# A hybrid decoder trunk on one core: the S5 stage's step list rewritten, with the gates and the first output products taken into it

## The chip, the cores and the metric

The kernel runs on one NeuronCore of a Trainium2 chip. The metric is device time in microseconds (us) of one execution; smaller is better. A core has five engines that run their own instruction queues in order: PE (TensorE, matrix products), ACT (ScalarE), DVE (VectorE), POOL (GpSimd) and SP (SyncE, which here only issues DMAs). They wait for one another through semaphores.

## What is computed

Two layers on a sequence of 256 tokens with 1024 channels, float32 throughout. Each layer is half a SwiGLU feed-forward, a mixer, and another half feed-forward. The mixer of layer 0 is an S5 state-space layer, that of layer 1 a block-sparse attention. The change is in the S5 mixer, cut here to what matters:

```python
u = h @ w_in                                   # 256 x 1024
# per group of 16 channels: 64 complex states, a diagonal recurrence over the 256 tokens
st = scan(lam, bb * u)                         # st[t] = lam * st[t-1] + bb u[t]
y = Re(c * st) + d_skip * u
g = gelu(y)
g = g * sigmoid(g @ w_glu)
return g @ w_out
```

The kernel computes the recurrence on every fourth token only (the tokens in between are folded into small tables), as a rotation, a real scan and a rotation back.

## The kernel before

The program runs six phases one after the other: `f00`, `s5`, `f01` (layer 0), `f10`, `moba`, `f11` (layer 1). Large products keep their precision by a split: every operand is written as a high part in the fast format fp32r plus a low part (the remainder), and a product is three matmuls: high by high, high by low, low by high (`mm3`, L398 to 401).

**Weights** come through the class `Stream`. A unit is 128x2048 floats in one of three raw buffers (L176, L182, L188 issue the loads on SP). `split` (L74 to 97) turns a half unit of 128x1024 into `whi` on ACT (L86) and `wlo` on DVE (L87), for units with gains in two pieces (L92, L93). There are 9 slots of `whi` and `wlo`. A call of `pump` splits the next half if its raw unit has been asked for and a slot is free; else it does nothing. `release` gives a slot back. When both halves of a unit are split, its raw buffer is free and SP issues the next load. Which pump splits what is thus fixed when the program is written out; at run time ACT and DVE take the splits in their queues' order.

**The S5 phase** works on eight blocks b of 128 channels. Its steps, with their names in the step list:

- `w<c0>.<t>:<k>` is `w_in`: one of 8 contraction steps of a product u = h @ w_in for column group c0 (256 columns for c0 = 0 and 256, 512 for c0 = 512) and token half t. With k = 7, ACT copies the sum from PSUM to `us` (L999) and DVE transposes it into `U` (L1000).
- `t<b>` is `t1`: 32 matmuls of 63 columns (L1009) that make block b's inputs of the scan in PSUM: in bank A0 to A3 for b < 4, in one of the two M buffers for b of 4 and above.
- `r<b>` is `rot`: two small ACT instructions (L1020, L1021), then on DVE four rotation products in place in PSUM (L1028 to 1031) and two scans (L1033), then on POOL four instructions (L1035 to 1038) that rotate back into `hr`.
- `y<b>` is `y_out`: 48 matmuls (L1052) from `U` and `hr`, then the gelu on ACT (L1056) and a transpose on DVE (L1058).
- `g<b>` is `g_tr`: two PE transposes (L1067). For b of 2 and above ACT writes the high part (L1070), DVE the low part (L1071), and ACT then a plain copy `gf` (L1072).
- `u<b>:<o>` is `glu`: block b's part of g @ w_glu for eight column blocks o (L1090 in plain float32 for b < 2, three fp32r matmuls L1092 to 1094 for the others). The sums are in the banks A0 to A3, two column blocks in each.
- `P` is one pump; `gelu` and `sigmoid` load the ACT table of that function (L234); `x` is a part of the phase's entry.

The list itself is `plan` (L1139 to 1146), written out by hand or by a planner; `step` (L1117 to 1135) runs a word of it. The order of the words is the order in every engine's queue.

**After the list** comes fixed code: for i = 0 to 3, `glu(6)` and `glu(7)` for the column blocks 2i and 2i+1 and then `gate(i)`. A gate reads the sum in bank Ai with a sigmoid (ACT, L1103), multiplies (DVE, L1105), writes the high part (ACT, L1107) and the low part (DVE, L1108). Then come the output products `so(b, t, n)` (L1110 to 1115, by `bank_mm` and `mm3`) for b = 0 and 1, with one or two pumps after each pair. `so(0, t, n)` begins a new sum in bank A(2t+n), the bank that gate 2t+n reads; `so(b)` takes the gated blocks 2b and 2b+1 that gate b writes. The products with b = 2 and 3, the residual sum (L371) and the transposes for the next phase are in `boundary` (L373 to 397).

Of the kernel before, what the change touches and what calls it, by code (L numbers as in the profile page):

```python
# [120 lines left out]
def trunk_kernel(ctx: ExitStack, tc, x, ffn_norm, ffn_w_gate, ffn_w_up, ffn_w_down, mix_norm,  # L121
# [20 lines left out]
    def psA(i):  # L142
        return pp.tile([128, 512], F32, name=f"pA{i}", tag=f"A{i}", bufs=1)
# [12 lines left out]
    where = {}  # L156
# [74 lines left out]
    def warm(func):  # L231

        w = sp.tile([128, 1], F32, name="warm", tag="warm", bufs=1)
        nc.scalar.activation(w, ones[:, 0:1], func)  # L234
# [33 lines left out]
    if "s5" in phases:  # L268
        rho = cp.tile([128, 32], F32, name="rho")
        tstack, lstack, xstack = ExitStack(), ExitStack(), ExitStack()  # L270
# [8 lines left out]
    st = Stream(nc, units, rp, hp)  # L279
# [20 lines left out]
    XP = [xp]  # L300
# [22 lines left out]
    def prep(t, n, ph, sq=True):  # L323

        if (ph, "x") not in X:
            X.clear()
            X[ph, "x"] = True
            X["h"], X["l"] = home(XP[0], ph)
        hh = h[t][:, n * 512:(n + 1) * 512]
        ps = psR()  # L330
        pv = ps.rearrange("p (k c) -> p k c", c=128)
        for k in range(4):
            nc.tensor.transpose(pv[:, k, :], hh[:, k * 128:(k + 1) * 128], ident)  # L333
        xh, xl = (X[p][:, n * 4:n * 4 + 4, t * 128:t * 128 + 128] for p in "hl")
        nc.scalar.activation(xh, pv, AF.Copy)
        nc.vector.tensor_tensor(xl, pv, xh.bitcast(F32), op=OP.subtract)
        if sq:
            squares(t, n)
# [80 lines left out]
    def bank_mm(acc, t, n, lh, ll, u, kks, first, last):  # L419

        for kk in kks:
            wh, wl = st.get(u, kk)
            c = slice(n * 512, n * 512 + 512)
            mm3(acc[2 * t + n], lh[:, kk, t * 128:t * 128 + 128], ll[:, kk, t * 128:t * 128 + 128],
                wh[:, c], wl[:, c], first and kk == kks[0], last and kk == kks[-1])
# [536 lines left out]
    def s5(nxt, entry):  # L962
        V, P = nc.vector, nc.gpsimd
        HALVES = (slice(0, 64), slice(64, 128))
        wstack = ExitStack()
# [16 lines left out]
        def w_in(c0, t, k):  # L982

            n = 512 if c0 >= 512 else 256
            if k == 0:
                W[c0, t] = psM()
            ps = W[c0, t]
            ts = slice(t * 128, t * 128 + 128)
            u = where["win", c0 // 512, k // 4]
            i = (k % 4) // 2  # L990
            wh, wl = st.get(u, i)
            c = (k % 2) * 512 + c0 % 512
            mm3(ps[:, 0:n], X["h"][:, k, ts], X["l"][:, k, ts], wh[:, c:c + n], wl[:, c:c + n], k == 0, k == 7)
            left[u, i] = left.get((u, i), 4 * (512 // n)) - 1
            if not left[u, i]:
                st.release(u, i)
            if k == 7:
                us = wp.tile([128, 512], F32, name="us", bufs=1)
                nc.scalar.activation(us[:, 0:n], ps[:, 0:n], AF.Identity, scale=Rr[t])  # L999
                V.transpose(U[:, c0 // 32:(c0 + n) // 32, t, :], us[:, 0:n].rearrange("p (q c) -> p q c", c=32))  # L1000
# [73 lines left out]
        def glu(b, os):  # L1074

            u = where["glu", b // 2]
            g = gf[b // 2][:, b % 2, :]
            if b < WHOLE:
                w = st.raw[u][:, b % 2 * 1024:b % 2 * 1024 + 1024]
            else:  # L1080
                gh, gl = GT["h"][:, b, :], GT["l"][:, b, :]
                wh, wl = st.get(u, b % 2)
            for o in os:
                first, last = b == 0 and o % 2 == 0, b == NB - 1
                if first:
                    acc[o // 2] = psA(o // 2)
                d = acc[o // 2][:, (o % 2) * 256:(o % 2) * 256 + 256]
                c = slice(o * 128, o * 128 + 128)
                if b < WHOLE:
                    mm(d, w[:, c], g, start=first, stop=last, skip_group_check=True)  # L1090
                else:
                    mm(d, wh[:, c], gh, start=first, stop=False, skip_group_check=True)  # L1092
                    mm(d, wh[:, c], gl, start=False, stop=False, skip_group_check=True)
                    mm(d, wl[:, c], gh, start=False, stop=last, skip_group_check=True)
                if o == 7 and b >= WHOLE:
                    st.release(u, b % 2)
                elif o == 7 and b % 2:
                    st.free_raw(u)

        def gate(i):  # L1100

            sg = fp.tile([128, 2, 256], F32, name="sg", tag="gr", bufs=2)
            nc.scalar.activation(sg, acc[i].rearrange("p (a c) -> p a c", a=2), AF.Sigmoid)  # L1103
            g = gf[i]
            V.tensor_tensor(g, g, sg, op=OP.mult)  # L1105
            gh, gl = (GT[p][:, 2 * i:2 * i + 2, :] for p in "hl")
            nc.scalar.activation(gh, g, AF.Copy)  # L1107
            V.tensor_tensor(gl, g, gh.bitcast(F32), op=OP.subtract)  # L1108

        def so(b, t, n, last=False):  # L1110
            u = where["so", b]
            if b == 0:
                acc[2 * t + n] = psA(2 * t + n)
            gh, gl = (GT[p][:, 2 * b:2 * b + 2, :] for p in "hl")
            bank_mm(acc, t, n, gh, gl, u, [0, 1], b == 0, last)

        def step(word):  # L1117
            name, _, ks = word.partition(":")
            ks = [int(k) for k in ks.split("-")] if ks else []
            ks = range(ks[0], ks[-1] + 1) if ks else ()  # L1120
            if name[0] == "w":
                c0, t = name[1:].split(".")
                for k in ks:
                    w_in(int(c0), int(t), k)
            elif name[0] == "u":
                glu(int(name[1]), ks)
            elif name == "x":
                if entry:
                    prep(1, 1, "s5")
            elif name == "P":  # L1130
                st.pump()
            elif name in ("gelu", "sigmoid"):
                warm(AF.Gelu_apprx_tanh if name == "gelu" else AF.Sigmoid)
            else:
                {"t": t1, "r": rot, "y": y_out, "g": g_tr}[name[0]](int(name[1]))

        plan = """  # L1139
            w0.0:0-1 P x w0.0:2-5 P w0.0:6 w0.1:0 w0.0:7 w0.1:1-4 P w0.1:5-7 w256.0:0-4 w256.1:0-1 t0 w256.0:5  # L1140
            w256.1:2 P w256.0:6 r0 w256.1:3 w256.0:7 P t1 w512.0:0 w256.1:4-7 w512.0:1 r1 w512.0:2-3 t2 gelu
            r2 t3 y0 w512.0:4-5 w512.1:0-1 w512.0:6 w512.1:2 r3 w512.1:3-4 w512.0:7 w512.1:5 y1 w512.1:6-7 g0
            y2 P P u0:0-1 g1 t4 u0:2-3 r4 g2 u0:4 t5 u0:5-7 r5 u1:0 t6 y3 u1:1-2 r6 u1:3-7 u2:0-2 t7 y4 g3
            u2:3-5 r7 y5 u2:6-7 u3:0-2 y6 g4 u3:3-4 g5 u3:5-7 P u4:0 P u4:1 P u4:2 g6 y7 u4:3-4 P P u4:5-7
            u5:0-1 sigmoid g7 u5:2-5 P u5:6-7 P
        """
        for word in plan.split():
            step(word)
        wstack.close()
        lstack.close()  # L1150
        XP[0] = xstack.enter_context(tc.tile_pool(name="xt2", bufs=1))
        for i in range(4):
            glu(6, (2 * i, 2 * i + 1))
            glu(7, (2 * i, 2 * i + 1))
            gate(i)
        for b in range(2):
            for t in range(2):
                for n in range(2):
                    so(b, t, n)
                if t == 1:  # L1160
                    for i in range(2):
                        st.release(where["so", b], i)
                st.pump(2 - b * t)

        boundary(nxt, [lambda t, n: so(2, t, n), lambda t, n: so(3, t, n, True)], acc, 1.0, pumps=(1, 2))
        for b in (2, 3):
            for i in range(2):
# [204 lines left out]
    v2, rn, r2 = (sp.tile([128, 2], F32, name=n, tag=n, bufs=1) for n in ("ms2", "rn2", "rr2"))  # L1372
# [41 lines left out]
    for i, ph in enumerate(phases):  # L1414
        nxt = phases[i + 1] if i + 1 < len(phases) else None
        if ph[0] == "f":
            if i:
                with tc.tile_pool(name="rows", bufs=1) as RP[0]:
                    ffn_w(ph, nxt, entry_hooks(ph))
            else:  # L1420
                ffn(ph, nxt, first, fill, to_rows, to_columns)
            if i and phases[i - 1] == "s5":
                xstack.close()
        else:
            if ph == "s5":
                st.aged = False
                for _ in tab:
                    slot[0] += 2.0
                s5(nxt, i > 0)
            else:  # L1430
                moba(nxt)
# [43 lines left out]
```

## Time and profile before

| What | Value |
|---|---|
| Median of three runs | 982.28 us (981.8 to 982.3) |
| The profiled execution: its own time | 982.36 us |
| Its span, first to last instruction | 980.4 us, so 1.96 us lie around it |
| DVE busy in the span | 688.8 us (70%) |
| ACT busy in the span | 560.4 us (57%) |
| POOL busy in the span | 186.5 us (19%) |
| First w_in matmul of the S5 phase, by the timeline | 213.48 us |
| First matmul of so(0) | 287.14 us |

Times in the views are counted from the span's start. A row of the timeline reads: start, duration, engine, source line, operation, tile written and tiles read, how many instructions were merged; a bracket gives the idle time of the engine just ahead and what ended it. Matmuls overlap, so what one costs PE is the distance from its start to the next start, not its duration.

### The profile page before, as it was taken

The numbers are of one execution on the slowest core, as the hardware profiler recorded it, in microseconds if no ns is written. First come the engines' busy times: TensorE is split into PE (matmuls) and PEld (weight loads), VectorE is DVE, ScalarE is ACT, GpSimd is POOL, SyncE is SP. The second block draws the span as 40 slices with busy tenths as digits, with TensorE's granted clock in tenths as the row PEclk, the third lists the DMA queues.
The fourth block names the chain that finished last, engine by engine and source line by source line (L and its number), as shares of the span: only waits on it lengthen the run. The fifth ranks groups of instructions, "written<-read, shape, count | busy, mean of one in ns | idle before, by whom it ended". The sixth has DMA issues, their size and how long they took to land.

```text
span 980.4 us, 17231 instructions
## 1 busy us (share of the span) xinstructions
PE 972.2 (99%) x6727; PEld 867.5 (88%) x6727; DVE 688.8 (70%) x1118; ACT 560.4 (57%) x1008; POOL 186.5 (19%) x364
## 2 busy tenths in 40 slices
PE   9999999999999999999999999999999999999998
PEld 7878888788888999999999999998788899999997
DVE  5799767768768676666667766665789667766662
ACT  7565766553267555555456655544897556655540
POOL 6963544416511000000010000000441010000000
PEclk9999999999999999999999999999999999999999
DMA  8988877887645666565536656562544546656531
GB/s 284 249 269 279 275 261 242 298 324 245 252 173 182 213 208 215 172 212 175 172 125 214 221 173 214 173 215 92 172 145 157 186 143 214 231 174 213 172 130 44
DMA packets 140002, 198.74 MB, mean 203 GB/s; under 512 B 18232, under 2 KB 111504, under 8 KB 139664
## 3 DMA queue, kind: packets, MB, share of 16 engines
q1 hardware_dynamic: 133808, 184.32, 57.5%
q0 software_dynamic: 5536, 12.71, 3.6%
q8 instruction: 53, 0.87, 0.4%
q10 hardware_dynamic: 576, 0.61, 0.3%
q14 instruction: 29, 0.24, 0.1%
HBM read 183.89 MB, written 13.66 MB: 202 GB/s over the span
## 4 chain that ended last, share of the span: by engine, by line
PE 94%; DVE 2%; ACT 2%; issue 1%; POOL 1%; DMA 1%; SPq 0%; POOLq 0%; DVEq 0%; ACTq 0%
PE pM L554 13%; PE pM L553 13%; PE pM L555 13%; PE pA L399 9%; PE pA L401 9%; PE pA L400 9%; PE pM L399 6%; PE pM L400 6%; PE pM L401 6%; PE pA L473 1%; PE pR L1052 1%; PE pR L333 1%; DVE wlo L87 1%; PE pA L1090 1%; PE pR L866 1%
## 5 line engine op out<-in xcount | busy, mean ns | idle before, releaser
L553 PE MATMUL pM<-xa,whi 128*128 128x256 f32 x1056 | 295.7, 280 | 0.0
L554 PE MATMUL pM<-xa,whi 128*128 128x256 f32 x1056 | 294.9, 279 | 0.0
L555 PE MATMUL pM<-xa,wlo 128*128 128x256 f32 x1056 | 294.7, 279 | 0.0
L93 DVE SCALAR_TENSOR_TENSOR wlo<-raw,gT,whi 128x512 fp32r<-128x512 f32 x328 | 228.1, 748 | 71.2 <-ACT whi L92 71.0
L87 DVE TENSOR_TENSOR wlo<-raw,whi 128x1024 fp32r<-128x1024 f32 (+1 forms) x155 | 187.5, 1225 | 56.0 <-ACT whi L86 54.8
L92 ACT ACTIVATE whi<-raw,gT 128x512 fp32r<-128x512 f32 x328 | 213.7, 711 | 16.4 <-PE pA L401 14.6
L554 PEld LDWEIGHTS pM<-xa,whi 128*128 128x128 f32 x1056 | 198.5, 188 | 2.6
L553 PEld LDWEIGHTS pM<-xa,whi 128*128 128x128 f32 x1056 | 198.5, 188 | 2.3
L555 PEld LDWEIGHTS pM<-xa,wlo 128*128 128x128 f32 x1056 | 198.5, 188 | 0.0
L86 ACT ACTIVATE whi<-raw 128x1024 fp32r<-128x1024 f32 (+1 forms) x155 | 158.7, 1049 | 26.1 <-DMA raw<-in_ffn_w_up_dram 9.8
L399 PE MATMUL pA<-whi,ah 128*128 128x512 f32 x352 | 138.8, 394 | 0.0
L400 PE MATMUL pA<-wlo,ah 128*128 128x512 f32 x352 | 137.6, 391 | 0.0
L401 PE MATMUL pA<-whi,al 128*128 128x512 f32 x352 | 137.6, 391 | 0.0
L568 ACT ACTIVATE sg<-gr 128x256 f32<-128x256 f32 x66 | 27.6, 418 | 165.7 <-DVE gr L565 165.7
L399 PE MATMUL pM<-whi,xa 128*128 128x512 f32 (+1 forms) x304 | 122.2, 402 | 0.0
L400 PE MATMUL pM<-wlo,xa 128*128 128x512 f32 (+1 forms) x304 | 115.8, 381 | 0.1
L401 PE MATMUL pM<-whi,xa 128*128 128x512 f32 (+1 forms) x304 | 115.5, 380 | 0.0
L348 POOL TENSOR_TENSOR ms<-ss 128x1 f32<-128x1 f32 x10 | 1.9, 193 | 470.3 <-ACT sq L345 470.3
L401 PEld LDWEIGHTS pA<-whi,al 128*128 128x128 f32 x352 | 66.1, 188 | 14.3
L399 PEld LDWEIGHTS pA<-whi,ah 128*128 128x128 f32 x352 | 66.1, 188 | 11.6
L400 PEld LDWEIGHTS pA<-wlo,ah 128*128 128x128 f32 x352 | 66.2, 188 | 11.3
L565 DVE TENSOR_TENSOR gr<-pM,rrow 128x512 f32<-128x512 f32 x66 | 45.5, 689 | 40.9 <-PE pM L555 40.8
(269 smaller groups left out, 1214.5 us busy)
## 6 DMA issues: line engine op xcount, KB each, us to landing
raw<-in_ffn_w_down_dram SPq DMA_DIRECT2D x44, 1024.0 KB, 5.4
raw<-in_ffn_w_gate_dram SPq DMA_DIRECT2D x80, 512.0 KB, 4.0
raw<-in_ffn_w_up_dram SPq DMA_DIRECT2D x80, 512.0 KB, 5.1
raw<-in_moba_w_qkv_dram SPq DMA_DIRECT2D x12, 1024.0 KB, 5.1
TB<-dB SPq DMA_DIRECT2D x8, 768.0 KB, 6.6
raw<-in_ffn_w_gate_dram SPq DMA_DIRECT2D x16, 256.0 KB, 4.4
raw<-in_ffn_w_up_dram SPq DMA_DIRECT2D x16, 256.0 KB, 4.7
dB<-tt POOLq DMA_DIRECT2D x16, 256.0 KB, 5.1
```

Of the source, the lines that this page charges most:

```text
L86: nc.scalar.activation(hi[:, c], r[:, c], AF.Copy)
L87: nc.vector.tensor_tensor(lo[:, c], r[:, c], hi[:, c].bitcast(F32), op=OP.subtract)
L92: nc.scalar.activation(hi[:, c], r[:, c], AF.Identity, scale=g)
L93: nc.vector.scalar_tensor_tensor(lo[:, c], r[:, c], g, hi[:, c].bitcast(F32), op0=OP.mult, op1=OP.subtract)
L399: mm(o, xh, wh, start=start, stop=False)
L400: mm(o, xh, wl, start=False, stop=False)
L401: mm(o, xl, wh, start=False, stop=stop)
L553: mm(o, a, xh, start=k == 0 and i == 0, stop=False, skip_group_check=True)
L554: mm(o, a, xl, start=False, stop=False, skip_group_check=True)
L555: mm(o, b, xh, start=False, stop=k == 7, skip_group_check=True)
L565: V.tensor_tensor(gr, ps.rearrange("p (i c) -> p i c", i=2), Rr["row"][:, None, :].to_broadcast([128, 2, 256]), op=OP.mult)
L568: nc.scalar.activation(sg, gr[:, 0, :], AF.Silu)
```

## The change

The step list is rewritten, and two new words join it: `a<i>` runs `gate(i)` (before the first, two memory pools are closed and one is opened, as the fixed code did), and `o<b>:<k>` runs `so(b, k // 2, k % 2)`, with the release of its slots after k = 3. The fixed code for `glu(6)`, `glu(7)`, the gates and `so(0)`, `so(1)` goes, since these are words now. The code of every step is as it was, and each step runs as often as before. The whole of the diff:

```diff
             elif name == "P":
                 st.pump()
+            elif name[0] == "a":
+                if name == "a0":
+                    wstack.close()
+                    lstack.close()
+                    XP[0] = xstack.enter_context(tc.tile_pool(name="xt2", bufs=1))
+                gate(int(name[1]))
+            elif name[0] == "o":
+                b = int(name[1])
+                for k in ks:
+                    so(b, k // 2, k % 2)
+                    if k == 3:
+                        for i in range(2):
+                            st.release(where["so", b], i)
             elif name in ("gelu", "sigmoid"):
                 warm(AF.Gelu_apprx_tanh if name == "gelu" else AF.Sigmoid)
...
         plan = """
-            w0.0:0-1 P x w0.0:2-5 P w0.0:6 w0.1:0 w0.0:7 w0.1:1-4 P w0.1:5-7 w256.0:0-4 w256.1:0-1 t0 w256.0:5
-            w256.1:2 P w256.0:6 r0 w256.1:3 w256.0:7 P t1 w512.0:0 w256.1:4-7 w512.0:1 r1 w512.0:2-3 t2 gelu
-            r2 t3 y0 w512.0:4-5 w512.1:0-1 w512.0:6 w512.1:2 r3 w512.1:3-4 w512.0:7 w512.1:5 y1 w512.1:6-7 g0
-            y2 P P u0:0-1 g1 t4 u0:2-3 r4 g2 u0:4 t5 u0:5-7 r5 u1:0 t6 y3 u1:1-2 r6 u1:3-7 u2:0-2 t7 y4 g3
-            u2:3-5 r7 y5 u2:6-7 u3:0-2 y6 g4 u3:3-4 g5 u3:5-7 P u4:0 P u4:1 P u4:2 g6 y7 u4:3-4 P P u4:5-7
-            u5:0-1 sigmoid g7 u5:2-5 P u5:6-7 P
+            w0.0:0-1 P x w0.0:2-5 P w0.0:6-7 w0.1:0-7 w256.0:0-1 P w256.0:2-3 P w256.0:4 w256.1:0 P t0
+            w256.0:5 w256.1:1 r0 w256.0:6 w256.1:2-6 w256.0:7 gelu t1 w512.0:0-2 w256.1:7 w512.0:3 w512.1:0 r1
+            w512.1:1 w512.0:4 t2 y0 t3 r2 w512.1:2-3 g0 w512.1:4 r3 w512.1:5 w512.0:5-6 y1 w512.1:6-7 u0:0-1
+            w512.0:7 u0:2 g1 u0:3 P u0:4 y2 t4 t5 P r4 u0:5-7 u1:0-2 g2 r5 y3 u1:3-5 t6 u1:6 r6 u1:7 u2:0-1 y4
+            t7 g3 u2:2-5 r7 y5 u2:6-7 u3:0 g4 u3:1-3 P u3:4-5 g5 y6 P u3:6-7 u4:0-5 P P y7 u4:6-7 u5:0 P g6
+            u5:1 P u5:2 g7 u5:3-7 sigmoid P u6:0-1 u7:0-1 a0 P u6:2-3 u7:2-3 a1 u6:4-5 u7:4-5 a2 P P u6:6-7
+            u7:6-7 a3 o0:0-1 P P o0:2-3 P P o1:0-1 P P o1:2-3 P
         """
         for word in plan.split():
             step(word)
-        wstack.close()
-        lstack.close()
-        XP[0] = xstack.enter_context(tc.tile_pool(name="xt2", bufs=1))
-        for i in range(4):
-            glu(6, (2 * i, 2 * i + 1))
-            glu(7, (2 * i, 2 * i + 1))
-            gate(i)
-        for b in range(2):
-            for t in range(2):
-                for n in range(2):
-                    so(b, t, n)
-                if t == 1:
-                    for i in range(2):
-                        st.release(where["so", b], i)
-                st.pump(2 - b * t)
-
         boundary(nxt, [lambda t, n: so(2, t, n), lambda t, n: so(3, t, n, True)], acc, 1.0, pumps=(1, 2))
```

## The prediction

> **What bounds the kernel now.** The page comes first: its span, its busy times, its chain.
>
> ```profile
> span 980.4 us, 17231 instructions
> PE 972.2 (99%) x6727; PEld 867.5 (88%) x6727; DVE 688.8 (70%) x1118; ACT 560.4 (57%) x1008; POOL 186.5 (19%) x364
> PE 94%; DVE 2%; ACT 2%; issue 1%; POOL 1%; DMA 1%; SPq 0%; POOLq 0%; DVEq 0%; ACTq 0%
> ```
>
> PE is busy nearly always and makes 94% of the chain that ended last. No step of the change alters the matmuls, so the time can move only by what PE waits in the S5 stage. The second view is the busy time by stretches: bounds and length in us, then PE, PEld, DVE, ACT, POOL with counts in brackets, the granted clock, the DMA share, GB/s.
>
> ```profile
> 224.00:225.00 1.00, 1.00 (x11) 1.00 (x10) 1.00 (x2) 0.21 (x1) 0.00 (x0) 1.00 0.34 70
> ...
> 270.00:280.00 10.00, 8.88 (x110) 8.47 (x109) 6.58 (x9) 7.26 (x14) 2.40 (x3) 1.00 0.42 150
> ...
> 290.00:304.00 14.00, 14.00 (x62) 11.32 (x62) 11.69 (x15) 9.33 (x13) 0.00 (x0) 1.00 0.48 145
> ```
>
> PE idles 1.12 us in the second of these stretches and not at all in the third (the first serves below). The third view, PE's timeline, has every wait of the stage above 0.1 us:
>
> ```profile
> 253.82 1.15 PE L1009 MATMUL pM<-U,TA 128*64 128x63 f32 x32 [0.33 <-issue]
> ...
> 278.55 0.41 PE L1067 MATMUL pR<-cst,gs 128*128 128x128 f32 x2 [1.12 <-DVE gs L1058]
> ...
> 281.37 0.28 PE L1093 MATMUL pA<-xa,whi 128*128 128x256 f32 x1
> 281.50 0.28 PE L1094 MATMUL pA<-xa,wlo 128*128 128x256 f32 x1
> 281.66 0.38 PE L1092 MATMUL pA<-xa,whi 128*128 128x256 f32 x1
> 282.12 0.39 PE L1093 MATMUL pA<-xa,whi 128*128 128x256 f32 x1
> ...
> 287.48 0.39 PE L400 MATMUL pA<-wlo,xa 128*128 128x512 f32 x1
> 287.87 0.50 PE L401 MATMUL pA<-whi,xa 128*128 128x512 f32 x1
> ...
> 291.40 0.39 PE L401 MATMUL pA<-whi,xa 128*128 128x512 f32 x1
> 291.63 0.48 PE L399 MATMUL pA<-whi,xa 128*128 128x512 f32 x1
> ```
>
> Brackets give the first two. The starts 281.66 and 282.12 stand 0.46 us apart, 287.48 and 287.87 0.39, where such matmuls follow each other at some 0.12 (281.37 to 281.50) and 0.23 (291.40 to 291.63), so about 0.34 and 0.16 are waits. Together 0.33 + 1.12 + 0.34 + 0.16 = 1.95 us: all that a better order could win, 0.2% of the time.
>
> The last row is the one to remember. At 291.63 PE begins so(0,1,1), word o0 with k = 3, in bank A3, which gate 3 must have read. The gates, from ACT's and DVE's timelines:
>
> ```profile
> 281.64 0.42 DVE L1071 TENSOR_TENSOR xa<-pR,xa 128x256 fp32r<-128x256 f32 x1 [0.38 <-ACT xa L1070]
> ...
> 283.46 2.36 DVE L87 TENSOR_TENSOR wlo<-raw,whi 128x1024 fp32r<-128x1024 f32 x2 [1.40 <-ACT whi L86]
> 285.74 0.68 DVE L1105 TENSOR_TENSOR gf<-gf,sg 128x512 f32<-128x512 f32 x1
> ```
>
> ```profile
> 281.24 0.36 ACT L1070 ACTIVATE xa<-pR 128x256 fp32r<-128x256 f32 x1
> 282.09 0.38 ACT L1072 ACTIVATE gf<-pR 128x256 f32<-128x256 f32 x1 [0.49 <-DVE xa L1071]
> 282.37 2.00 ACT L86 ACTIVATE whi<-raw 128x1024 fp32r<-128x1024 f32 x2
> 284.27 0.59 ACT L1103 ACTIVATE sg<-pA 128x512 f32<-128x512 f32 x1
> 286.45 0.63 ACT L1107 ACTIVATE xa<-gf 128x512 fp32r<-128x512 f32 x1 [1.59 <-DVE gf L1105]
> 286.99 0.58 ACT L1103 ACTIVATE sg<-pA 128x512 f32<-128x512 f32 x1
> ...
> 290.98 0.58 ACT L1103 ACTIVATE sg<-pA 128x512 f32<-128x512 f32 x1
> ```
>
> The four sigmoids start between 284.27 and 290.98, the last ends at 291.56, and PE needs it at 291.63. **The gates are a serial chain of ACT and DVE with no slack left**: sigmoid, product, high part, next sigmoid. Without a split inside, a gate takes 2.0 us (286.99 to 290.98 is two of them).
>
> **The change part by part.** *Matmuls:* none is added or removed. *Splits:* I followed slots and raw buffers through both lists by the rules of the stream. Every P of the new list down to o0 finds a half to split; two of the last three find no slot. What matters is the place. Before, so(2) and so(3) are split behind all four gates. Now one half (so2) stands between gates 0 and 1 and two (so2, so3) between gates 2 and 3, in ACT's and DVE's queues ahead of the sigmoids. *DMAs:* the same loads, each still issued when a raw buffer comes free; those of the last units move with their splits.
>
> *The gates* (the largest term). One whi holds ACT 0.95 us start to start (282.37 to 284.27 is two), one wlo starts 1.09 us behind its whi (282.37 to 283.46) and holds DVE 1.14 (283.46 to 285.74 is two). Inside a gate, product to high part is 0.71, high part to next sigmoid 0.54, which leaves 0.74 of the 2.0 from sigmoid to product. Between gates 0 and 1: 0.95 for the whi, less 0.19 because one split and not two now stands right ahead of gate 0's product (it comes 0.14 + 1.14 behind the sigmoid, not 1.47): +0.76. Between gates 1 and 2: gate 1's product waits for that wlo, at whi + 1.09 + 1.14, where its sigmoid alone would allow whi + 0.95 + 0.74: +0.54. Between gates 2 and 3: two whi, 1.90. Sum 3.2 us: from the first sigmoid's start to the last's 9.9 us, not 6.7.
>
> *When gate 0 starts.* Queue costs for this come from ACT and DVE ahead of the gates, and from the first unhurried y and u on PE:
>
> ```profile
> 264.90 0.69 DVE L1028 TENSOR_TENSOR wv<-pM,TE 128x512 f32<-128x512 f32 x1 [0.52 <-ACT pM L1020]
> 268.44 0.42 DVE L1058 STREAM_TRANSPOSE gs<-yg 128x256 f32<-128x256 f32 x1
> ...
> 273.40 3.50 DVE L87 TENSOR_TENSOR wlo<-raw,whi 128x1024 fp32r<-128x1024 f32 x3 [1.40 <-ACT whi L86]
> 276.81 0.42 DVE L1071 TENSOR_TENSOR xa<-pR,xa 128x256 fp32r<-128x256 f32 x1
> ```
>
> ```profile
> 279.83 1.28 ACT L234 ACT_TABLE_LOAD   x1
> ```
>
> ```profile
> 244.79 0.34 PE L1052 MATMUL pR<-U,TB 128*64 128x64 f32 x4
> ...
> 246.34 1.13 PE L1090 MATMUL pA<-gf,raw 128*128 128x256 f32 x4
> 247.31 0.38 PE L1067 MATMUL pR<-cst,gs 128*128 128x128 f32 x2
> ```
>
> A rotation holds DVE 3.54 us (264.90 to 268.44), a wlo 1.14 (3.41 for three), the table load with its first use 1.41 (279.83 to 281.24); a y takes PE 1.55 (244.79 to 246.34; I take 1.40 before another small-tile step), two u0 words 0.97. Before, y2 begins at 244.79. The new list has moved only u0:0-4 and g1 ahead of it: 5 x 0.48 + 0.3 (g1's row, 0.38, less its overlap), so y2 begins at 247.5 and ends at 248.9. Then DVE is the queue that fills: gelu, whi and wlo of the P behind t5 (0.2 and 0.3 for the hand-over and the gelu, then 1.09 + 1.14) put r4 at 251.65. Four rotations follow, 14.2 us, with two transposes, two low parts and ACT's hand-overs between them (an estimate from the 0.42 us of such rows: 0.9 + 0.4 + 1.3): r7 ends at 268.4. That is where it ended before, so the new order of t, r and y wins nothing at this point. From there, start times on the new list:
>
> | ACT | DVE |
> |---|---|
> | gf4 269.2, whi 269.5 | gs5 268.4, low part 4 268.75 |
> | gf5 272.5, gelu 6 272.8 | wlo 270.9, low part 5 272.05 |
> | three whi 273.05, 274.0, 275.0 | three wlo 274.15, 275.3, 276.45 |
> | gelu 7 276.0, whi 276.3, high part 6 277.3 | gs7 277.6, wlo 278.0, low part 6 279.15 |
> | gf6 279.6, whi 279.9, high part 7 280.9 | wlo 281.0, low part 7 282.15 |
> | gf7 282.6, table 282.9, whi 284.3, **sigmoid 0 285.25** | wlo 285.4, product 0 286.5 |
>
> Each gf waits for its block's low part (the 281.64 and 282.09 rows), and each low part now stands behind a wlo. On PE the last matmuls of gate 0's sum wait for low part 7 (282.15 + 0.42), then five of 0.12 and the last one's 0.28 follow: 283.4. So ACT is late, not PE. Gate 0 starts 285.25 - 284.27 = **1.0 us** later.
>
> One row in that table was bounded. The wlo at 270.9 meets POOL's work of r7. The nearest rows:
>
> ```profile
> 227.80 2.09 DVE L87 TENSOR_TENSOR wlo<-raw,whi 128x1024 fp32r<-128x1024 f32 x1
> ```
>
> ```profile
> 228.77 2.17 POOL L1036 TENSOR_TENSOR pv<-zo,TE 128x512 f32<-128x512 f32 x1
> ...
> 233.90 1.19 POOL L1035 TENSOR_TENSOR pv<-zo,TE 128x512 f32<-128x512 f32 x1 [1.46 <-issue]
> ...
> 237.01 0.74 POOL L1038 TENSOR_TENSOR hr<-pv,pv 128x256 f32<-128x256 f32 x1
> ```
>
> A wlo at 227.80, beside POOL products, took 2.09 us instead of 1.14, and the POOL product of 228.77 took 2.17 instead of 1.19: each waited for the other's whole instruction. Bounds are 0 and 0.95; by its place near the end of a POOL product I take 0.35, which the table holds. The Trainium skill has the rule, "SBUF — State Buffer", Who interferes with whom: a DVE instruction with both inputs in SBUF and a GpSimd one that reads SBUF share a port, and the second to come is blocked until the first ends. The trace agrees (2.09 and 2.17); the sum by the rule is the one above. A second rule speaks against the place of `sigmoid` behind g7. "ScalarE: Activation LUTs", What ACT_TABLE_LOAD costs, gives a switch about 2.66 us with a drain; the row has 1.41 to the next instruction. By the page gate 0 would start 1.25 us later still; the row decides.
>
> *The front.* The P ahead of t0 splits the first half of glu1, one position earlier than before:
>
> ```profile
> 219.37 0.37 SPq L182 DMA_DIRECT2D raw<-in_s_w_glu_dram  x1
> ```
>
> ```profile
> 226.01 1.05 ACT L86 ACTIVATE whi<-raw 128x1024 fp32r<-128x1024 f32 x1
> ```
>
> Its load is issued at 219.37 and its first use was at 226.01, so it lands in between; ACT would ask for it at 222.8 and hold r0 behind it. The DMA engines fall quiet at 224 (0.34 busy, 70 GB/s, in the stretch row above), so I take 224.1: whi, then wlo (1.09 + 1.14), then r0 from 226.3 (3.54) and POOL's four instructions (233.90 to 237.75 is 3.85): hr0 is there at 233.8, as PE comes to y0 by the new list (an estimate, 233.9). Price 0 if so, up to 1.9 us if the load lands only at 226.0. Fewer changes between small and full tiles (11 groups of t and y, not 12) save some 0.3 us on PE ahead of the gates, hidden under their wait.
>
> **The sum.** 1.0 + 3.2 = 4.2 us. PE begins o0 with k = 3 at about 295.75, not 291.63; its waits at u7, o0:0 and o0:2 fall inside that. Behind it everything is PE's, and PE comes 4.2 us later to work that is ready. So 982.36 + 4.2 = **986.6 us**; the median stands 0.08 us below the profiled run, which I leave.
>
> **The rivals.** *Front late:* the load of glu1 lands at 226.0, y0 waits 1.9 us, and r4 and all behind it move too: 982.36 + 4.2 + 1.9 = 988.5. Against it speaks the quiet of the DMA engines. *Gate 0 on time for PE:* ACT and DVE are ahead, and sigmoid 0 starts when PE has its sum, 283.4; then 9.9 + 0.6 to the end of sigmoid 3, 293.9, and 2.3 us are lost: 984.7. *The splits are not there:* if the P words between the gates find nothing to split, only the 1.0 us is left: 983.4; the bookkeeping of slots speaks against it. *The other side, faster:* the new order takes PE's four waits away, 1.95 us, and the gates keep up: 980.4. It decides at sigmoid 3, which must end by 291.56, so sigmoid 0 must start by 281.1 with the splits between. Before, PE had that sum at 282.9 (282.12, four more matmuls, the last one's end) with 0.33 + 1.12 + 0.34 us of waits ahead of it: without any of them 281.1. PE would just make it, and ACT, which by the table comes four us later, would not.
>
> **How the numbers follow.** Forecast 0.62 (own range 985.4 to 987.8, a gate start 1.2 us off either way), front late 0.13, gate 0 on time 0.13, no splits 0.05, faster 0.07. A measurement of this kernel can tell about 0.2%, 1.96 us, from no change, so 980.4 is at that bound and 983.4 within it. Faster 0.06, same 0.07, slower 0.87. The range 984.0 to 989.0 takes in the forecast, front late and gate 0 on time, and leaves out some 0.15.
>
> **What would show it.** After the change the last two sigmoid rows (L1103) should be about 4 us apart with two whi rows between them, sigmoid 0 near 285, and PE should idle some 4 us in all between 280 and 297, the longest time ahead of the first matmul in bank A3, with ACT as releaser. PE should be as busy as before up to y7. The prediction is wrong if the sigmoids follow each other at 2 us, if sigmoid 0 starts before 283, or if PE's long wait is at y0.

## The result and the profile after

The changed kernel takes 987.56 us (median of 6 runs, 986.47 to 988.30) where the kernel before takes 982.28 us: the ratio is 1.0052, with a 95% interval of 1.0040 to 1.0063. It is slower by 5.3 us. The forecast was 986.6 us with a range of 984.0 to 989.0.

The page of the profiled execution (987.44 us):

```profile
span 985.5 us, 17228 instructions
PE 974.1 (99%) x6727; PEld 867.8 (88%) x6727; DVE 688.8 (70%) x1118; ACT 560.6 (57%) x1008; POOL 188.3 (19%) x364
PE 85%; DVE 5%; ACT 3%; POOL 2%; issue 2%; DMA 2%; SPq 0%; DVEq 0%; ACTq 0%; POOLq 0%
```

DVE and ACT do the same amount of work as before (688.8 and 560.4 us then). The chain that ended last runs over DVE and ACT for more of the span. "Busy" hides most of the loss: PE's busy time grew by 1.9 us too, though no matmul was added. That is the first sign that some matmuls took longer.

Where PE stands still, by its timeline (with the matmuls behind the last wait):

```profile
280.55 0.38 PE L1092 MATMUL pA<-xa,whi 128*128 128x256 f32 x1 [0.18 <-ACT xa L1070]
...
287.26 0.50 PE L399 MATMUL pA<-whi,xa 128*128 128x512 f32 x1 [0.32 <-ACT xa L1107]
...
291.22 0.50 PE L399 MATMUL pA<-whi,xa 128*128 128x512 f32 x1 [0.68 <-ACT sg L1103]
...
295.10 0.61 PE L399 MATMUL pA<-whi,xa 128*128 128x512 f32 x1 [2.25 <-ACT sg L1103]
295.51 0.63 PE L400 MATMUL pA<-wlo,xa 128*128 128x512 f32 x1
295.94 0.63 PE L401 MATMUL pA<-whi,xa 128*128 128x512 f32 x1
...
298.85 0.40 PE L399 MATMUL pA<-whi,xa 128*128 128x512 f32 x1
```

The wait of 2.25 us at 295.10 is the one forecast: so(0,1,1) in bank A3, released by ACT's sigmoid. Then comes what was not forecast. Eight matmuls from 295.10 on start 0.43 us apart, and 0.23 again only once 298.85 is reached (those in between are left out). ACT's timeline has the reason for the wait:

```profile
281.85 0.38 ACT L1072 ACTIVATE gf<-pR 128x256 f32<-128x256 f32 x1 [1.35 <-DVE xa L1071]
282.24 1.28 ACT L234 ACT_TABLE_LOAD   x1
...
283.64 1.04 ACT L86 ACTIVATE whi<-raw 128x1024 fp32r<-128x1024 f32 x1
284.59 0.58 ACT L1103 ACTIVATE sg<-pA 128x512 f32<-128x512 f32 x1
...
287.12 1.04 ACT L86 ACTIVATE whi<-raw 128x1024 fp32r<-128x1024 f32 x1
288.06 0.58 ACT L1103 ACTIVATE sg<-pA 128x512 f32<-128x512 f32 x1
...
290.59 0.58 ACT L1103 ACTIVATE sg<-pA 128x512 f32<-128x512 f32 x1
...
292.58 1.99 ACT L86 ACTIVATE whi<-raw 128x1024 fp32r<-128x1024 f32 x2
294.47 0.58 ACT L1103 ACTIVATE sg<-pA 128x512 f32<-128x512 f32 x1
```

The whi rows (L86) stand between the sigmoids (L1103). From the first sigmoid to the last it is 9.88 us, where it was 6.71. The view by stretches, column 8 being the clock that PE was granted, explains the slow matmuls:

```profile
292.00:295.00 3.00, 0.85 (x4) 0.38 (x2) 2.04 (x4) 2.96 (x4) 0.00 (x0) 1.00 0.02 5
295.00:297.00 2.00, 1.90 (x5) 1.50 (x6) 1.61 (x2) 0.40 (x2) 0.00 (x0) 0.59 0.48 122
297.00:299.00 2.00, 2.00 (x6) 1.57 (x6) 1.44 (x2) 2.00 (x4) 0.00 (x0) 0.56 0.97 314
299.00:301.00 2.00, 2.00 (x11) 1.63 (x10) 2.00 (x4) 2.00 (x4) 0.00 (x0) 1.00 0.42 117
```

PE was busy 0.85 of 3 us, and in the two stretches behind that the granted clock is 0.59 and 0.56 on average. In stretches of half a microsecond it is 0.50 from 295.5 to 298.5, with a part of the stretch on either side: 3.4 us in all at half the clock.

**Reading a stage instead of a run.** Times of whole runs scatter by 1 us and more. The S5 stage can be measured in each trace by itself: from the first w_in matmul (the first row of PE that writes bank M there) to the first transpose for the next phase (L333). What follows that transpose takes 676.3 to 676.5 us in every one of the fourteen traces, and what precedes the stage, the same code in all of them, scatters from 212.82 to 214.10 us. So the stage is where the differences that the kernels make must lie. In the kernel before the stage goes from 213.48 to 304.05, 90.57 us; after the change from 212.90 to 309.08, 96.18 us. That is **+5.61 us**. Rows of two kernels are therefore to be compared after taking off the stage's start.

| Part of the +5.61 us | From | us |
|---|---|---|
| Gate 0's sigmoid starts later | 284.27 - 213.48 = 70.79 before; 284.59 - 212.90 = 71.69 after | 0.90 |
| First to last sigmoid | 6.71 before; 9.88 after | 3.17 |
| Matmuls at the low clock | 8 x (0.43 - 0.23) | 1.6 |

These make 5.67.

### The profile page after: what moved, and what is told of

Its sections match the earlier page's. It is cut to its first block, busy times and chain, and to the rows that moved or that the text cites. A ratio compares the mean times of both kernels' runs of the same rounds, so it can differ in the third digit from the quotient of the medians.

```text
span 985.5 us, 17228 instructions
## 1 busy us (share of the span) xinstructions
PE 974.1 (99%) x6727; PEld 867.8 (88%) x6727; DVE 688.8 (70%) x1118; ACT 560.6 (57%) x1008; POOL 188.3 (19%) x364
## 4 chain that ended last, share of the span: by engine, by line
PE 85%; DVE 5%; ACT 3%; POOL 2%; issue 2%; DMA 2%; SPq 0%; DVEq 0%; ACTq 0%; POOLq 0%
PE pM L553 13%; PE pM L554 13%; PE pM L555 13%; PE pA L399 9%; PE pA L400 9%; PE pA L401 9%; PE pM L399 4%; PE pM L400 4%; PE pM L401 4%; DVE wlo L87 2%; ACT whi L86 1%; DMA raw<-in_ffn_w_up_dram 1%; PE pR L333 1%; POOL qrs L306 1%; PE pR L866 1%
## 5 line engine op out<-in xcount | busy, mean ns | idle before, releaser
L86 ACT ACTIVATE whi<-raw 128x1024 fp32r<-128x1024 f32 (+1 forms) x155 | 159.1, 1049 | 27.2 <-DMA raw<-in_ffn_w_up_dram 9.5
```

Source lines behind the costliest of these rows:

```text
L86: nc.scalar.activation(hi[:, c], r[:, c], AF.Copy)
```

## The experiments

Theory A is the one on record: the chain of the gates, with three splits put into it, sets when PE may use bank A3. Rival B is that the new order of the t, r, y and u steps costs the time. C and D are two readings of the slow matmuls: that PE's clock falls because PE stood idle (C), or that ACT, DVE and the DMAs work beside them (D). The table has what came out; stage is the length defined above, and sigmoids are the starts of gates 0 and 3, counted from the stage's start, in us. The ratio is to the kernel before as it ran beside the kernel of the row; it took 982.28, 982.47, 982.61 and 982.73 us there, so medians of different rows can differ by some 0.4 us for that alone.

| Kernel | Median us (runs) | Ratio to before, 95% | Stage | Sigmoids |
|---|---|---|---|---|
| before | 982.28 (6) | | 90.57 | 70.79, 77.50 |
| after | 987.56 (6) | 1.0052 [1.0040, 1.0063] | 96.18 | 71.69, 81.57 |
| late_all | 983.47 (11) | 1.0012 [1.0003, 1.0021] | 91.28 | 71.77, 78.28 |
| late_two | 985.17 (7) | 1.0028 [1.0017, 1.0039] | 93.11 | 71.57, 79.57 |
| late_one | 985.33 (6) | 1.0030 [1.0018, 1.0043] | 93.52 | 72.04, 80.44 |
| old_head | 987.47 (5) | 1.0047 [1.0034, 1.0059] | 95.36 | 70.67, 80.75 |
| fill | 988.14 (5) | 1.0056 [1.0042, 1.0070] | 96.26 | 72.24, 82.12 |
| fill8 | 986.96 (5) | 1.0040 [1.0028, 1.0053] | 94.60 | 71.64, 81.53 |
| after_again | 988.39 (5) | 1.0057 [1.0044, 1.0069] | 96.31 | 71.76, 81.65 |
| o_order | 984.47 (11) | 1.0021 [1.0012, 1.0030] | 92.50 | 71.64, 81.53 |
| late_sig | 983.70 (11) | 1.0010 [1.0001, 1.0019] | 91.11 | 70.96, 77.48 |
| best1 | 981.27 (11) | 0.9988 [0.9979, 0.9996] | 89.28 | 69.55, 76.26 |
| best2 | 980.68 (11) | 0.9980 [0.9971, 0.9989] | 88.55 | 68.81, 75.52 |
| best3 | 980.77 (11) | 0.9981 [0.9972, 0.9990] | 88.19 | 68.42, 75.12 |

### The head or the tail of the list

**late_all** takes the splits out from between the gates.

```diff
-            u5:1 P u5:2 g7 u5:3-7 sigmoid P u6:0-1 u7:0-1 a0 P u6:2-3 u7:2-3 a1 u6:4-5 u7:4-5 a2 P P u6:6-7
+            u5:1 P u5:2 g7 u5:3-7 sigmoid P u6:0-1 u7:0-1 a0 u6:2-3 u7:2-3 a1 u6:4-5 u7:4-5 a2 u6:6-7
```

> The changed kernel with its three splits taken out from between the gates: the pumps behind gates 0 and 2 are dropped, those behind o0 and o1 do the work, as before. Theory A (the gates' chain): the three splits cost 3.2 us and the long wait of PE, with the slow clock behind it, 1.6 more; both go, only gate 0's later start (0.9) is left: about 982.8 us, sigmoids 2.0 us apart, granted clock 1.0 throughout. Rival B (the new order of the t, r, y and u steps costs the time): the time stays near 987.5.

Measured: 983.47 us, 0.7 us more than expected; the stage is 4.90 us shorter than after the change (4.8 was expected), but it starts at 213.61 and not at 212.90. The sigmoids in its ACT timeline:

```profile
285.38 0.58 ACT L1103 ACTIVATE sg<-pA 128x512 f32<-128x512 f32 x1
...
287.90 0.58 ACT L1103 ACTIVATE sg<-pA 128x512 f32<-128x512 f32 x1
...
289.89 0.58 ACT L1103 ACTIVATE sg<-pA 128x512 f32<-128x512 f32 x1
...
291.89 0.58 ACT L1103 ACTIVATE sg<-pA 128x512 f32<-128x512 f32 x1
```

They are 2.0 us apart again, except the first pair (2.5, a wlo is still ahead of gate 0's product). All the new order of t, r, y and u is still in this kernel, and it is 0.7 us of stage behind the kernel before, with gate 0 0.98 us later. Rival B falls as the main cause.

**old_head** is the counterpart: the old list up to its last word, and behind it, in place of the fixed code, the new tail.

```diff
             u5:0-1 sigmoid g7 u5:2-5 P u5:6-7 P
+            u6:0-1 u7:0-1 a0 P u6:2-3 u7:2-3 a1 u6:4-5 u7:4-5 a2 P P u6:6-7
+            u7:6-7 a3 o0:0-1 P P o0:2-3 P P o1:0-1 P P o1:2-3 P
```

> The step list of before up to its last word, then the changed kernel's tail with one split between gates 0 and 1 and two between gates 2 and 3. Theory A: gate 0 starts as before and the three splits cost 3.3 us: 985.6 us, and 987.2 if the slow clock comes as well. Rival B: as before, 982.3.

Measured: 987.47 us. Gate 0 starts as before (70.67), the sigmoids span 10.08 us, and the clock falls:

```profile
293.00:295.00 2.00, 0.00 (x0) 0.00 (x0) 1.75 (x3) 2.00 (x3) 0.00 (x0) 1.00 0.00 0
295.00:297.00 2.00, 1.86 (x6) 1.52 (x7) 1.65 (x2) 0.40 (x2) 0.00 (x0) 0.77 0.41 110
297.00:299.00 2.00, 2.00 (x6) 1.54 (x5) 1.40 (x2) 2.00 (x4) 0.00 (x0) 0.50 0.91 264
299.00:301.00 2.00, 2.00 (x9) 1.61 (x9) 2.00 (x4) 2.00 (x4) 0.00 (x0) 0.88 0.60 181
```

The new tail alone is worth 4.79 of the 5.61 us. Of the five runs one took 985.37 us, with a mean clock of 0.999; the other four took 987.1 to 987.6, with 0.998.

### What each split costs

**late_two** drops the two pumps behind gate 2 (first pair of lines), **late_one** the one behind gate 0 (second pair).

```diff
-            u5:1 P u5:2 g7 u5:3-7 sigmoid P u6:0-1 u7:0-1 a0 P u6:2-3 u7:2-3 a1 u6:4-5 u7:4-5 a2 P P u6:6-7
+            u5:1 P u5:2 g7 u5:3-7 sigmoid P u6:0-1 u7:0-1 a0 P u6:2-3 u7:2-3 a1 u6:4-5 u7:4-5 a2 u6:6-7
...
-            u5:1 P u5:2 g7 u5:3-7 sigmoid P u6:0-1 u7:0-1 a0 P u6:2-3 u7:2-3 a1 u6:4-5 u7:4-5 a2 P P u6:6-7
+            u5:1 P u5:2 g7 u5:3-7 sigmoid P u6:0-1 u7:0-1 a0 u6:2-3 u7:2-3 a1 u6:4-5 u7:4-5 a2 P P u6:6-7
```

> The changed kernel without the two pumps between gates 2 and 3; the one behind gate 0 stays. Theory A: the two high parts cost 1.9 us of the chain and are gone, and with PE's wait ahead of bank A3 down from 2.25 to some 0.5 us the clock does not fall (1.6): about 984.0 us. If the clock falls all the same: 985.6. Rival B: 987.5.

> The changed kernel without the pump behind gate 0; the two between gates 2 and 3 stay. Theory A: 1.3 us of the chain are gone; PE reaches bank A3 earlier too and still waits there about 2 us at a stretch: about 986.2 us if the clock falls behind that wait as before, 984.7 if it does not. Rival B: 987.5.

Measured: 985.17 and 985.33 us. The sigmoids span 8.00 and 8.40 us, so the two splits behind gate 2 hold the chain 1.88 us (9.88 - 8.00; 1.90 was worked out) and the one behind gate 0 1.48. The 1.30 worked out for that one is not the same quantity: it is 0.95 + 0.54 less the 0.19 that one split fewer ahead of gate 0's product saves, and this edit leaves that saving in place. 0.95 + 0.54 = 1.49 is what to hold against 1.48; the 0.19 shows in late_all, where the sigmoids span 6.51 us and not 6.71. late_two came 1.2 us above its expectation: 0.4 of it in the stage (93.11, expected 96.18 - 1.9 - 1.6 = 92.7) and 0.6 ahead of it (it starts at 213.51, not 212.90). late_one came 0.6 us above its expectation for a clock that does not fall, and its trace starts the stage 0.67 us later (213.57). PE stands 1.70 us at bank A3 there, where it was 2.25 in the kernel after the change, and the clock behind it stays up:

```profile
294.64 0.50 PE L399 MATMUL pA<-whi,xa 128*128 128x512 f32 x1 [1.70 <-ACT sg L1103]
...
295.44 0.39 PE L399 MATMUL pA<-whi,xa 128*128 128x512 f32 x1
295.67 0.39 PE L400 MATMUL pA<-wlo,xa 128*128 128x512 f32 x1
```

### The slow matmuls

**fill** and **fill8** put idle work on PE ahead of the first matmul in bank A3, into a bank that is not read: 16 matmuls of ones by ones, 128x128, in fill, and `busy(8)` in fill8.

```diff
                 for k in ks:
+                    if (b, k) == (0, 3):
+                        busy(16)
                     so(b, k // 2, k % 2)
```

> The changed kernel with 16 small matmuls of ones by ones put on PE ahead of the first matmul in bank A3, into a bank that nothing reads; they take about 1.9 us and lie in PE's wait of 2.25. Theory C (the clock falls because PE stood idle): PE is kept busy, the granted clock stays at 1.0 between 295 and 299, so the eight matmuls behind the wait follow at 0.23 and not 0.43 us: about 985.9 us. Rival D (those matmuls are slow because ACT, DVE and DMAs work beside them): they stay at 0.43 and the time near 987.5.

> The changed kernel once more, beside the three kernels that follow. If the slow clock behind PE's wait comes in some executions and not in others, its times fall into two groups some 1.6 us apart, near 986 and near 987.6; if it always comes, they lie within 1 us of 987.6.

> As the kernel with 16 filler matmuls, but with 8 of them: there they took 3.49 us, more than the wait of 2.25 that they were to fill, so 8 should take 1.75 and lie in it. Theory C (the clock falls because PE stood idle): granted clock 1.0 behind the wait, no time added by the filler: 1.6 us less than the changed kernel where that one falls, about 986.0. Rival D (the matmuls behind the wait are slow because of ACT, DVE and DMAs): 987.6.

Measured: with 16 the clock stays at 1.00 between 293 and 301 us, but the filler takes 3.49 us, so it delays the first matmul in bank A3 by 1.1 us (297.37, the sigmoid having ended at 296.23): 988.14 us. The count was wrong, and the time says nothing. With 8 (each leaves two records in the trace, so the row counts 16):

```profile
293.86 1.95 PE L1370 MATMUL pR<-ones 128*128 128x128 f32 x16
296.26 0.50 PE L399 MATMUL pA<-whi,xa 128*128 128x512 f32 x1 [0.46 <-ACT sg L1103]
296.60 0.39 PE L400 MATMUL pA<-wlo,xa 128*128 128x512 f32 x1
296.82 0.39 PE L401 MATMUL pA<-whi,xa 128*128 128x512 f32 x1
```

The sigmoids stand where they stood (71.64 and 81.53), ACT, DVE and the DMAs do the same work, and the matmuls behind the wait follow at 0.23 us. The stage is 94.60 us, 1.7 less than in after_again on the same chip, the time 1.43 less (986.96 and 988.39). It is 1.0 us above the 986.0 expected; after_again, the same kernel as after, is 0.8 above 987.56 on this chip too. So the cause is PE's own idling (C), not the work of others (D). after_again has one run of five at 987.36 us with a mean clock of 1.000 and four from 988.18 to 989.09 with 0.998; in the first six runs it was two, 986.47 and 986.71, with 1.000, and four from 987.44 to 988.30 with 0.998. By these means the clock falls in 8 of 11 executions, not in all.

### Is it bank A3?

**o_order** leaves every split where the change put it and gives PE other products to do while gate 3 is late.

```diff
-            u7:6-7 a3 o0:0-1 P P o0:2-3 P P o1:0-1 P P o1:2-3 P
+            u7:6-7 a3 o0:0-1 P P o0:2 o1:0-2 P P o0:3 P P o1:3 P
```

> The changed kernel with another order of the output products: o0:0-2, o1:0-2, o0:3, o1:3, so that PE has three products to do while gate 3 is late; all splits stay where they are between the gates. Theory A: PE's wait at bank A3 goes and with it the slow clock, 2.25 + 1.6 us: about 983.7 us. If the splits cost time in another way than by holding bank A3 (contention), the time stays at 986 to 987.5.

Measured: 984.47 us. The last sigmoid is as late as in the changed kernel (81.53), and the list of PE's waits from 283 to 300 us is short:

```profile
PE pA L399 <- ACT sg L1103: 0.7, 1, 0.7
PE pA L399 <- ACT xa L1107: 0.3, 1, 0.3
```

3.7 us of stage come back without moving one split (2.25 + 1.6 were expected; the time is 0.8 above the expectation, and the stage starts 0.6 us later, at 213.50). So this part of the loss is not contention: it is PE's wait for the bank. The stage is still 1.93 us longer than before the change. In it PE's busy time falls 2.86 us short of the stage's length, 1.52 before: the two rows above, 0.9 us at u7 for block 7's low part, and 0.26 at the stage's end among them. The rest is not taken apart.

### Gate 0's start, and a list that beats both

**late_sig** is late_all with the sigmoid's table load moved one word ahead of g7.

```diff
-            u5:1 P u5:2 g7 u5:3-7 sigmoid P u6:0-1 u7:0-1 a0 u6:2-3 u7:2-3 a1 u6:4-5 u7:4-5 a2 u6:6-7
+            u5:1 P u5:2 sigmoid g7 u5:3-7 P u6:0-1 u7:0-1 a0 u6:2-3 u7:2-3 a1 u6:4-5 u7:4-5 a2 u6:6-7
```

> The changed kernel with the splits out from between the gates, and the table load of the sigmoid one step earlier, ahead of g7, as it stood before. If gate 0's later start (0.9 us against before) is the load's new place, behind block 7's last copy and ahead of the next split, it goes: the load then overlaps the wlo that block 7's low part waits for, gate 0 starts 0.9 us earlier and the time is about 982.6. If it has to do with the order of the rotations, the time stays at 983.5.

Measured: gate 0 starts 0.81 us earlier (70.96, not 71.77), so the load's place is the cause of its delay. The time does not follow (983.70 us, the stage only 0.17 us shorter): the load now stands ahead of block 7's high part, and PE's wait has moved there, to 1.7 us at u7:

```profile
PE pA L1092 <- ACT xa L1070: 1.7, 1, 1.7
```

Three kernels build on the old list, with the gates as before. **best1** moves one split to where DVE was idle (the P behind u3:5-7 goes behind r6), **best2** a second one (the P behind u4:0 goes behind r7), and **best3**, shown here with all three edits, also gives PE one more word of work ahead of t6.

```diff
-            y2 P P u0:0-1 g1 t4 u0:2-3 r4 g2 u0:4 t5 u0:5-7 r5 u1:0 t6 y3 u1:1-2 r6 u1:3-7 u2:0-2 t7 y4 g3
-            u2:3-5 r7 y5 u2:6-7 u3:0-2 y6 g4 u3:3-4 g5 u3:5-7 P u4:0 P u4:1 P u4:2 g6 y7 u4:3-4 P P u4:5-7
+            y2 P P u0:0-1 g1 t4 u0:2-3 r4 g2 u0:4 t5 u0:5-7 r5 u1:0-1 t6 y3 u1:2 r6 P u1:3-7 u2:0-2 t7 y4 g3
+            u2:3-5 r7 P y5 u2:6-7 u3:0-2 y6 g4 u3:3-4 g5 u3:5-7 u4:0-1 P u4:2 g6 y7 u4:3-4 P P u4:5-7
```

> The step list of before with one pump moved: the second half of glu1's follower (glu2) is split behind r6, where DVE is idle, and no longer between u3 and u4. By theory A's way of counting, gelu 7 then stands behind two splits and not three: the wait of 1.12 us ahead of g7 goes down to some 0.1 and the gates start 1.0 us earlier: about 981.3 us. If the wlo meets POOL's work of r6 and holds y6 up, the gain is eaten: 982.3.

> As best1, and the first half of glu3 is split behind r7 as well, not between u4:0 and u4:1. It meets POOL's work of r7, so hr7 comes about 1.1 us later and y7 may wait 0.4; for that g7 has no wait and the gates start another 0.9 us earlier: about 980.8 us. If y7's wait is longer than 1 us: 981.5 to 982.5.

> The list of before with two splits moved up behind r6 and r7, and one more u word (u1:1) put ahead of t6, where PE waited 0.33 us for the scans of r4: 0.3 us less than with the two splits alone, about 980.4 us. If the word only moves the wait to y3: 980.7.

Measured: 981.27, 980.68 and 980.77 us. best1 and best2 came where they were expected. best2's wlo does meet POOL's product of r7, as the prediction's rule has it (2.02 us instead of 1.19):

```profile
267.88 2.02 POOL L1035 TENSOR_TENSOR pv<-zo,TE 128x512 f32<-128x512 f32 x1 [1.73 <-issue]
```

PE's only wait in best2 is the one at t6:

```profile
PE pM L1009 <- issue: 0.3, 1, 0.3
```

y7 did not have to wait. In best3 PE has no wait at all in the stage; its stage is 0.36 us shorter than best2's, but the medians of the runs do not tell the two apart. best2 beats the kernel before by 0.2% (0.9980, 0.9971 to 0.9989), about the 1.95 us of waits that the prediction put up as the most that an order could win. That bound was a little low, though: by the stage best2 wins 2.02 us and best3 2.38, and by these views PE's busy time in the stage is 0.98 us lower in best3 than before (88.07 and 89.05), so some of what an order wins is counted as busy.

## Why the prediction was right

The direction and the mechanism were right, by the steps on record.

- *The gates, 3.2 us.* Measured 3.17 (9.88 against 6.71), and late_two and late_one show its parts: 1.88 for 1.90, and 1.48 for 0.95 + 0.54; the 0.19 that comes off again shows in late_all. With the three splits gone (late_all) PE's wait at bank A3 is gone too.
- *Gate 0 later by 1.0 us.* Measured 0.90. The walk along ACT's and DVE's queues held at its marks, once the stage's earlier start by 0.58 us is taken off: r7 ends at 268.4 in the walk and at 267.94 + 0.58 = 268.52 in the trace, sigmoid 0 starts at 285.25 and at 285.17. late_sig shows that the place of the table load makes this delay.

```profile
267.94 0.42 DVE L1058 STREAM_TRANSPOSE gs<-yg 128x256 f32<-128x256 f32 x1
...
270.06 1.50 DVE L87 TENSOR_TENSOR wlo<-raw,whi 128x1024 fp32r<-128x1024 f32 x1 [1.40 <-ACT whi L86]
```

- *The wlo beside POOL, 0.35 us.* From its start to DVE's next it took 1.43 us (270.06 to 271.49) instead of 1.14: 0.29. The row's 1.50 is a duration, to be held against the 1.23 of the wlo at 280.26, which has no POOL product beside it: 0.27. The prediction's bound of 0.95 mixes the two in the same way (a duration of 2.09 with a distance of 1.14); like with like it is 0.87.
- *The front at no price* holds for the rows it names. The first half of glu1 was split when its load landed, and y0 begins with no wait:

```profile
223.82 1.06 ACT L86 ACTIVATE whi<-raw 128x1024 fp32r<-128x1024 f32 x1 [1.49 <-DMA raw<-in_s_w_glu_dram]
```

  223.82 + 0.58 = 224.4, against the 224.1 that was read off the DMA engines' quiet. One small wait of the front was not foreseen: PE stands 0.26 us at 230.63 for ACT's copy `us`. No cost of it shows at the gates either, where ACT is what comes late.
- *PE as busy as before up to y7* was not quite right: bank R holds y6 up (0.29 us in the trace, released by block 4's copy gf), because r7 is still on DVE and block 4's low part behind it. It lies ahead of the gates, where ACT is later still, and no cost of it shows in gate 0's start. PE's listed waits between 280 and 297 us come to 0.18 + 0.94 + 0.32 + 0.68 + 2.25 = 4.37, where some 4 were named.
- *Behind bank A3 "everything is PE's" with nothing added* is the step that failed. The granted clock fell to half behind the wait, and eight matmuls took 1.6 us more; the sum has no term for that. The stage's +5.61 us against the forecast's 4.2 are this 1.6 and small differences. In the runs in which the mean clock stayed at 1.000 the changed kernel took 986.47 and 986.71 us, the forecast almost to the digit; the median, 987.56, is of those in which it fell. To the digit is luck: what precedes the stage scatters by more than 1 us, and the run of after_again in which the mean clock stayed at 1.000 took 987.36 on its chip. That the median lies in the range without the clock's term owes something to the range's width.

The rival on the other side decided where it was said to: at the end of sigmoid 3, which came 4.07 us too late (295.05 - 212.90 against 291.56 - 213.48). The three rivals that were no worse than the forecast (front late, gate 0 on time, no splits) are out by the rows above.

## What to carry to other kernels

An engine that is 30 or 40% idle on average can still hold a serial chain with no slack: find the chain whose last link PE consumes without a gap, and count what any moved work puts into its queues ahead of the links. Where a bank must be read out before it is used anew, let the consumer begin with banks that are free and give it other products in the meantime: that took back 3.7 of 5.6 us here without moving any split. A wait on PE of about 2 us can cost more than its length, so it is worth shortening or filling.

## What the runs showed of the hardware

The granted TensorE clock fell to 0.50 behind a wait of PE of 2.2 us. Three profiles show it (after, after_again, old_head, with waits of 2.25, 2.23 and 2.25 us). In each the clock fell 0.2 to 0.9 us after PE had taken up work again, and it stayed at 0.50 for 3.4 us, by stretches of half a microsecond. By the mean clock of the runs (0.998) it fell in four of six and four of five runs of the changed kernel and in four of five of old_head. It did not behind 1.70 us in late_one (mean clock 0.999 or more in all six runs). The Trainium skill, "TensorE: Matmul & The Clock Gate", Part 1, puts the fall after an idle window of about 3.4 us. The time at the low clock here is as long as that window, but the window need not be empty: in the 3.4 us ahead of each fall PE stood still for 2.2 us and worked for 1.2. That the phase of such a window against the wait decides which runs fall would fit, but no run here shows it. Three of the eleven runs of late_sig, with its 1.7 us at u7, also had a mean clock of 0.997 or 0.998 and took 984.7 to 985.3 us; no profile was taken of those, so whether it is the same effect stays open.
